# Decoder block on eight cores: spare PSUM banks for projections, more output buffers, a new memory map for one of two programs, and a shared prefix

## The chip, the cores and the metric

The kernel runs on all 8 cores of one Trainium2 chip, in one launch. Cores 0 to 3 are one die, cores 4 to 7 the other. The time is device microseconds (us) of the slowest core, as the median of several executions. In some executions one die is granted a lower TensorE clock and the run is 2 to 17% longer; such runs are slow. Means by core use fast runs alone; the plain medians include the slow runs.

## The reference

One layer on a residual stream `x` of 4 sequences of 4096 tokens and 1024 channels. Cut to what matters:

```python
u = rms_norm(x, norm_mix)
q, k, v, z, g_att, g_pool = split(u @ w_in)       # q, k, v: 24 heads of 64 each
q, k = partial_rope(q), partial_rope(k)
att = dilated_attention(q, k, v)                  # windows 128, 512, 2048 with dilations 1, 4, 16;
                                                  # groups combined by softmax denominators
pooled = multiscale_pool(z) @ w_pool_group * pool_scale
merged = sigmoid(g_att) * (att @ w_att_branch) + sigmoid(g_pool) * (pooled @ w_pool_branch)
h = x + merged @ w_out
f = rms_norm(h, norm_ffn)
h = h + (silu(f @ w_ffn_gate) * (f @ w_ffn_up)) @ w_ffn_down
return rms_norm(h, norm_final)
```

Two cores share a sequence. The even core takes tokens 0 to 2127, the odd core the other 1968, for which it recomputes keys and values of a history.

## The kernel before

The two halves are two programs, `First` (even cores) and `Second` (odd cores), each a list of instructions per engine. They are in one binary, and every engine branches on a flag at its start:

```python
def both(eng, e=e):
    v = eng.value_load(flag)
    with eng.If(v > 0):
        progs[1].body(eng, e)        # Second
    with eng.Else():
        progs[0].body(eng, e)        # First
```

The lists are written by an emitter with its own timing model. Each instruction moves its engine's modelled clock on, and the next unit of TensorE work is the one that can start first by that model. ScalarE's modelled cost:

```python
def act(out, in_, func, **kw):
    ...
    return P.op("act", ..., (width(in_) / 1200 + 0.11, 0.08))   # us busy, us until visible
```

PSUM has eight banks. During attention the scores have banks 0 to 3, the attention outputs 4 and 5, and the projections of the next head pair, which fill TensorE's gaps, only 6 and 7:

```python
pj = dict(banks=tuple(range(8)))

def bank():
    return PSB[min(pj["banks"], key=lambda i: P.ready("pe", [], [PSB[i]]))]
...
        pj["banks"] = (6, 7)                 # when scores are emitted
...
        pj["banks"] = (6, 7, 0, 1, 2, 3)     # after the last scores
```

The FFN runs in two passes over the tokens. The final norm of the first pass's tokens, and its output, are tasks that are interleaved with the second pass: `c2` takes two tasks per FFN step. The outputs go through four staging buffers:

```python
def norm_tasks(cols, sq, ps, rs, fin):
    ...
    return out + [lambda: None] * 8 + [root] + [lambda c=c: fin(cols, rs, c) for c in range(8)]

def emit_out(slots, queues=("sp",)):
    def f(cols, rs, c):
        o = slots[C["o"] % len(slots)][:, 0:cols.stop - cols.start]
        C["o"] += 1
        stt(o, ht[c][:, cols], cstv[:, 16 + c:17 + c], rs, ALU.mult, ALU.mult)
        P.outs.append(P.dma(queues[C["o"] % len(queues)], T["oT"][c * 128:(c + 1) * 128, cols], o, more=True))
    return f
...
ost = [f32(K.OST + i * K.FN, K.FN) for i in range(4)]
...
for i, cols in enumerate(FP[0]):
    tasks += norm_tasks(cols, K.SQB, PSB[4 + i % 2], rs2[i % 2], eo)
c2(1, tasks)                                 # pop(tasks, 2) after each step of 16 matmuls
```

SBUF is one tile, `arena`, cut by hand: each program is a class of offsets. [...]

The softmax here doesn't subtract the row's maximum and nothing guards it: scores larger than these inputs give would overflow.

Of the kernel before, what the change touches and what calls it, by code (L numbers as in the profile page):

```python
# [18 lines left out]
NFIRST = 2128  # L19
NW = 53152  # L20
GRAN = 32
# [4 lines left out]
class First:  # L26
# [10 lines left out]
    RPIECE = ((0, 532, 1064),) * 3  # L37
    NMSK = 2016
    GT = (432, 432, 432, 416, 416)
    FP = ((352, 352, 352), (352, 352, 368))  # L40
    TAILS = (192, 176)
    FN, PW = 368, 1072
    UTH, UTO, ATT = None, 8544, 17056
    CST, MSK, ONE = 21312, 21440, 22464
    QK = ((0, 2128, 4256), (22528, 24656, 26784)) * 2
    VS = (28912, 30544, 32176)
    ACC, ACT_ = 33808, 37904
    PT = 38064
    WP = 40112
    TAB = (44720, 45784, 46848)  # L50
    XR = (47912, 48976, 50040)
    TT = 51104
    XS = ((ATT, ATT + 2048), (ACC, ACC + 2048), (22528, 24576), (26624, 6400), (VS[2], 0))
    SQP = (PT, XR[0]) * 2 + (PT,)
    RSP0 = TT
    NTS = (6400,) * 3 + (22528,)
    POOLT = 0
    ZB, ZS, ZT16, ZRUN = 4272, 448, 8368, (45488, 45920, 46352)
    ZW, WPG, WPGS = WP, 45232, 7856
    MERGED = 28912  # L60
    HT = (4288, 6416, 22528, 24656, 26784, 46768, 48896, 51024)
    RING = (42160, 43696, 40112)
    SIGS = (38064, 39088, 46848, 47872, 48896, 49920, 50944, 51968)
    WO = (37424, 41648, MSK, MSK + 512, 45488, 46000, 40112, 40624)
    WO_LATE = 2
    ACTT, RS2, FT = 8544, 20336, 0
    WGU = (38064, 42160, 44208)
    WDX = (28912, 31728, 0, 42160)
    SQA, SQB, SQC = 17760, 34544, 2816
    SIL, OST, OSL = 36016, 40112, 38064  # L70

class Second:
# [10 lines left out]
    RPIECE = ((0, 528, 1056), (0, 576, 1152), (0, 512, 1024, 1536))  # L83
    NMSK = 1024
    GT = (496, 496, 496, 480)
# [3 lines left out]
    UTH, UTO, ATT = 0, 8192, 16384  # L89
    CST, MSK, ONE = 20480, 20608, 21120  # L90
    QK = ((21184, 23296, 29152),) * 4
    VS = (25600, 27232, 32224)
# [16 lines left out]
    RING = (43488, 45024, 41440)  # L109
    SIGS = (39392, 40416, 47008, 48032, 49056, 50080, 51104, 52128)  # L110
    WO = (37344, 37856, 38368, 38880, 27328, 27840, 28352, MSK)
# [4 lines left out]
    SQA, SQB, SQC = ACTT + 18 * 512, 27328, 2816  # L116
    SIL, OST, OSL = 29376, 30400, 43488

# [13 lines left out]
class Prog:  # L132
# [181 lines left out]

    def body(self, eng, e):
        for waits, fn, inc in self.ops[e]:
            for s, v in waits:
                eng.wait_ge(s, v)
            if fn is not None:
                ins = fn(eng)  # L320
                if inc is not None:
                    ins.then_inc(inc[0], inc[1])

def emit(nc, progs, flag):
    with nc.Block() as block:
        for e, deco in (("pe", block.tensor), ("act", block.scalar), ("dve", block.vector),
                        ("pool", block.gpsimd), ("sp", block.sync)):
            def both(eng, e=e):
                v = eng.value_load(flag)  # L329
                with eng.If(v > 0):  # L330
                    progs[1].body(eng, e)
                with eng.Else():
                    progs[0].body(eng, e)

            deco(both)
# [65 lines left out]
def _body(P, T, AR, PS, K):  # L401
    PSB = [PS[:, i * 512:(i + 1) * 512] for i in range(8)]

    def f32(off, n):
        return AR[:, off:off + n]

    def bf(off, n):
        return AR[:, off:off + n // 2].bitcast(BF16)
# [40 lines left out]
    eps = cstv[:, 96:97]  # L449
    mskv = [bf(K.MSK + i * 256, 512) for i in range(3 - K.HF)]  # L450
    onev = bf(K.ONE, 128)
# [49 lines left out]
    for i in range(2):  # L501
        load_piece(1, i)
    for k in range(2, 4):
        load_x(k)

    def load_consts(q, tabs):
# [4 lines left out]
        if 0 in tabs:  # L511
            P.dma(q, bf(K.MSK, K.NMSK), T["msk"][:, 0:K.NMSK])

    if not K.HF:
# [4 lines left out]
        load_consts("pool", (2,))  # L519
    memset(onev, 1.0)  # L520
    act(f32(K.PT, 1), onev[:, 0:1], AF.Square)
    for i in range(WARM):
        mm(PSB[7][:, 0:128], onev, onev, True, True)

    def ones(g):
# [10 lines left out]

    for g in range(2):
        ones(g)
        if K.HF:
            pads(g)  # L540

    pj = dict(banks=tuple(range(8)))

    def bank():
        return PSB[min(pj["banks"], key=lambda i: P.ready("pe", [], [PSB[i]]))]

# [3 lines left out]
    def norm(k):  # L550
# [5 lines left out]
        for a, b in K.PIECES[k]:  # L556
# [7 lines left out]
            def stat(a=a, b=b, n=n):  # L564
                ps = bank()[:, 0:n]

                def emit():
# [11 lines left out]
                    if not K.HF:  # L579
                        if k == 4:  # L580
                            ones(2)
                        return
# [227 lines left out]
    def scores(sp, qi):  # L810
# [5 lines left out]
        def finish():  # L816
            if n == 4 * NS - 1:
                pj["banks"] = (6, 7, 0, 1, 2, 3)
            done(("s", n), *[("S", sp, k) for k in closes])

        def make():
# [4 lines left out]
            def emit():  # L826
                pj["banks"] = (6, 7)
                for a, (b, pb, _) in enumerate(quad):
# [14 lines left out]
        def make_tail():  # L843
            def emit():
                pj["banks"] = (6, 7)
                for g, kb_, cols, c0_ in tail_parts():
# [6 lines left out]
                for lo, nk in ((0, 128), (240, 80)):  # L853
                    src = PS[0:nk, 0:1024].rearrange("p (e c) -> p e c", e=2)[:, :, lo:lo + 240]
                    v = pts[0][0:nk].rearrange("p (e c) -> p e c", e=2)[:, :, lo:lo + 240]
                    act(v, src, AF.Exp, scale=0.125)
                    mk = bf(K.MSK + 768, 480)[0:nk, lo:lo + 240]
                    tt(v, v, mk.unsqueeze(1).broadcast_to([nk, 2, 240]), ALU.mult)
# [206 lines left out]
    wo = [bf(o, 1024).rearrange("p (c n) -> p c n", c=8) for o in K.WO]  # L1065
    sigv = [[f32(o + k * 512, 512) for k in range(2)] for o in K.SIGS]
    sfree, sused = list(range(len(K.SIGS))), {}

# [36 lines left out]
    def load_wo(dcs):  # L1105
        for dc in dcs:
            P.dma("pool", bf(K.WO[dc], 1024), T["wout"][dc])

    def mixed(i):
        dc, tg = divmod(i, NG)  # L1110
# [21 lines left out]
    while mi < total:  # L1132
        n = 2 if gi - mi > 1 or gi == total else 1
        if gi < total:
# [7 lines left out]
        if not loaded and max(sused.values()) < 2:  # L1142
            loaded = True
            for c in range(8):
                if K.HF:
                    P.dma("sp", ht[c][:, 0:1536].rearrange("p (g t) -> p g t", g=3), xhv[c][:, 4:7, :])
                    P.dma("sp", ht[c][:, 1536:K.T], xhv[c][:, 7, 0:K.OWN[3]])
                else:
                    P.dma("sp", ht[c][:, 0:2048].rearrange("p (g t) -> p g t", g=4), xhv[c][:, 4:8, :])
                    P.dma("sp", ht[c][:, 2048:K.T], T["xt"][:, c * 80:c * 80 + 80])  # L1150
            load_wo(range(8 - K.WO_LATE))

    actt = bf(K.ACTT, NJ * K.PW).rearrange("p (j t) -> p j t", j=NJ)
# [4 lines left out]
    sil = [f32(K.SIL + i * K.FN, K.FN) for i in range(2)]  # L1158
    ost = [f32(K.OST + i * K.FN, K.FN) for i in range(4)]
    FP = [spans(K.FP[0]), spans(K.FP[1], sum(K.FP[0]))]  # L1160
# [115 lines left out]
    for i, cols in enumerate(FP[0]):  # L1276
        tasks += norm_tasks(cols, K.SQB, PSB[4 + i % 2], rs2[i % 2], eo)
    c2(1, tasks)
# [4 lines left out]
    hw = max(K.TAILS)  # L1283
    halves = [[f32(o + i * hw, hw) for i in range(8)] for o in (K.OST, K.OSL)]
    parts = FP[1][:-1] + spans(K.TAILS, FP[1][-1].start)
# [144 lines left out]
```

## Time and profile before

| | us |
|---|---|
| median of 5 runs (lowest, highest) | 1162.27 (1161.22, 1281.11) |
| spans of even cores 0, 2, 4, 6 in the profiled run | 1163.1, 1159.5, 1159.7, 1157.4 |
| spans of odd cores 1, 3, 5, 7 in the profiled run | 1155.2, 1156.5, 1156.6, 1157.8 |
| mean span over 28 fast runs in the three later sessions, even and odd cores | 1158.1 and 1157.2 |

How to read the lines: PE is TensorE's matmul side, ACT is ScalarE, DVE is VectorE, and an evacuation is a copy out of PSUM by one of these two; `SPq` is the queue on which SyncE issues transfers. A row of the time line gives start, duration, engine, source line, operation, output and input; the bracket at its end gives the idle time of the engine before it and what ended it. Most instructions go through small helpers, so a line number names the helper: L425, L434, L439, L443 and L420 before are L432, L441, L446, L450 and L427 after (ScalarE, two of VectorE, the memset, the matmul). The page's sums are of the slowest core, which is core 0 before.

### The profile page before, as it was taken

The numbers are of one execution on the slowest core, as the hardware profiler recorded it, in microseconds if no ns is written. First come the engines' busy times: TensorE is split into PE (matmuls) and PEld (weight loads), VectorE is DVE, ScalarE is ACT, GpSimd is POOL, SyncE is SP. The second block draws the span as 40 slices with busy tenths as digits, with TensorE's granted clock in tenths as the row PEclk, the third lists the DMA queues.
The fourth block names the chain that finished last, engine by engine and source line by source line (L and its number), as shares of the span: only waits on it lengthen the run. The fifth ranks groups of instructions, "written<-read, shape, count | busy, mean of one in ns | idle before, by whom it ended". The sixth has DMA issues, their size and how long they took to land.

```text
span 1163.1 us, 23864 instructions; the slowest of 8 cores (1155.2 to 1163.1 us)
## 1 busy us (share of the span) xinstructions
PE 1107.8 (95%) x9246; PEld 725.4 (62%) x9246; DVE 525.4 (45%) x918; ACT 430.4 (37%) x788; POOL 64.9 (6%) x126
## 2 busy tenths in 40 slices
PE   4999989989999999999999999999999999899997
PEld 3666649538647755555556666666666665566677
DVE  2533584553384598544347822222354342332244
ACT  2744765553763775222223221211221343231122
POOL 4020000000000000100000000000000000000000
PEclk9999999999999999999999999999999999899999
DMA  6885335155035406852103074343443454340522
GB/s 128 261 158 134 92 76 110 17 104 137 11 72 123 78 1 140 206 134 41 19 1 73 8 166 73 74 76 70 74 85 66 86 123 81 84 118 5 97 75 79
DMA packets 41736, 103.36 MB, mean 89 GB/s; under 512 B 5712, under 2 KB 13008, under 8 KB 37648
## 3 DMA queue, kind: packets, MB, share of 16 engines
q0 software_dynamic: 16992, 63.57, 29.5%
q1 hardware_dynamic: 23328, 36.89, 10.9%
q8 instruction: 78, 1.28, 0.5%
q10 hardware_dynamic: 1296, 1.28, 0.4%
q14 instruction: 42, 0.34, 0.1%
HBM read 136.67 MB, written 18.52 MB: 133 GB/s over the span
## 4 chain that ended last, share of the span: by engine, by line
PE 82%; DMA 8%; DVE 3%; issue 3%; ACT 3%; SPq 1%; POOL 0%; POOLq 0%; DVEq 0%; ACTq 0%
PE ps_all L420 82%; DVE arena L434 3%; ACT arena L425 3%; DMA arena<-wd 2%; DMA arena<-sb 1%; DMA sa<-arena 1%; DMA sb<-arena 1%; SPq L306 1%; DMA arena<-xs 1%; DMA oT<-arena 1%; DMA arena<-sa 1%; DVE arena L439 0%; POOL arena L306 0%; POOLq L329 0%; DVE arena L472 0%
## 5 line engine op out<-in xcount | busy, mean ns | idle before, releaser
L420 PE MATMUL ps_all<-arena 128*128 128x352 bf16 (+12 forms) x9246 | 1107.8, 283 | 48.5 <-ACT arena L425 25.9
L420 PEld LDWEIGHTS ps_all<-arena 128*128 128x128 bf16 (+2 forms) x9246 | 725.4, 102 | 430.8 <-issue 72.7
L425 ACT ACTIVATE arena<-ps_all 128x512 bf16<-128x512 f32 (+8 forms) x530 | 296.3, 586 | 515.0 <-PE ps_all L420 479.9
L434 DVE TENSOR_TENSOR arena<-arena 128x1024 bf16<-128x1024 bf16 (+13 forms) x334 | 220.5, 670 | 150.6 <-ACT arena L425 114.4
L434 DVE TENSOR_TENSOR arena<-ps_all,arena 128x352 bf16<-128x352 f32 (+5 forms) x220 | 129.2, 594 | 294.5 <-PE ps_all L420 294.3
L425 ACT ACTIVATE arena<-arena 128x352 f32<-128x352 f32 (+13 forms) x222 | 109.7, 512 | 123.9 <-DVE arena L434 100.3
L439 DVE SCALAR_TENSOR_TENSOR arena<-arena 128x352 bf16<-128x352 f32 (+10 forms) x183 | 88.0, 533 | 55.0 <-ACT arena L425 40.8
L439 DVE SCALAR_TENSOR_TENSOR arena<-arena,ps_all 128x432 f32<-128x432 f32 (+1 forms) x80 | 47.2, 597 | 79.9 <-PE ps_all L420 77.3
L425 ACT ACT_TABLE_LOAD x15 | 19.2, 1283 | 59.6 <-PE ps_all L420 48.6
L306 POOL DMA_DIRECT2D arena<-wgu x22 | 11.6, 528 | 372.6 <-PE ps_all L420 325.0
L306 POOL DMA_DIRECT2D arena<-wq x36 | 19.3, 546 | 221.7 <-PE ps_all L420 210.6
L439 DVE SCALAR_TENSOR_TENSOR arena<-ps_all,arena 128x352 f32<-128x352 f32 (+1 forms) x48 | 24.5, 521 | 10.0 <-PE ps_all L420 10.0
L472 DVE CAST arena<-ps_all 80x128 bf16<-80x128 f32 (+3 forms) x20 | 7.5, 374 | 32.0 <-PE ps_all L420 32.0
L306 POOL DMA_DIRECT2D arena<-wb x24 | 12.7, 532 | 162.8 <-PE ps_all L420 162.8
L425 ACT ACTIVATE arena<-ps_all,arena 128x352 f32<-128x352 f32 (+7 forms) x21 | 10.8, 514 | 28.5 <-PE ps_all L420 28.4
L1040 DVE TENSOR_TENSOR_SCAN arena<-arena 128x432 f32<-128x432 f32 (+1 forms) x15 | 16.5, 1103 | 0.9 <-ACT arena L425 0.4
L306 POOL DMA_DIRECT2D arena<-wd x8 | 4.2, 529 | 121.6 <-PE ps_all L420 121.4
L443 DVE MEMSET arena<- 128x16 f32 (+3 forms) x9 | 3.4, 379 | 7.9 <-issue 7.4
L306 POOL DMA_DIRECT2D arena<-tab x6 | 3.4, 570 | 42.5 <-DMA arena<-tab 42.5
L306 POOL DMA_DIRECT2D arena<-wout x8 | 4.2, 553 | 14.8 <-PE ps_all L420 14.8
L306 POOL DMA_DIRECT2D arena<-wz x1 | 0.5, 527 | 73.1 <-PE ps_all L420 73.1
L306 POOL DMA_DIRECT2D arena<-xT x8 | 4.3, 639 | 0.0
(11 smaller groups left out, 8.1 us busy)
## 6 DMA issues: line engine op xcount, KB each, us to landing
arena<-wgu POOLq DMA_DIRECT2D x22, 1024.0 KB, 8.1
arena<-wd POOLq DMA_DIRECT2D x8, 1408.0 KB, 11.2
arena<-wq POOLq DMA_DIRECT2D x36, 256.0 KB, 6.0
arena<-xT SPq DMA_DIRECT2D x8, 1024.0 KB, 11.6
oT<-arena SPq DMA_DIRECT2D x40, 176.0 KB, 1.9
arena<-sa SPq DMA_DIRECT2D x12, 532.0 KB, 4.2
arena<-wb POOLq DMA_DIRECT2D x24, 256.0 KB, 5.4
arena<-xT POOLq DMA_DIRECT2D x8, 512.0 KB, 26.5
```

Source lines behind the costliest of these rows:

```text
L306: self.ops[q].append((waits, lambda e: e.dma_start(out=out, in_=in_), (sem, 16)))
L420: return P.op("pe", lambda e: e.matmul(out, lhsT=lhsT, rhs=rhs, start=start, stop=stop, **kw), [lhsT, rhs], [out], (busy, 0.17))
L425: return P.op("act", lambda e: e.activation(out=out, in_=in_, func=func, **kw), rd, [out], (width(in_) / 1200 + 0.11, 0.08))
L434: return P.op("dve", lambda e: e.tensor_tensor(out=out, in0=in0, in1=in1, op=op), [in0, in1], [out], cost_dve(out, in0, in1))
L439: return P.op("dve", lambda e: e.scalar_tensor_tensor(out=out, in0=in0, scalar=scalar, in1=in1, op0=op0, op1=op1), rd, [out], (width(out) ...
L443: return P.op("dve", lambda e: e.memset(out, v), [], [out])
L472: P.op("dve", lambda e: e.tensor_copy(out=dst, in_=src), [src], [dst], cost_dve(dst, src))
L1040: P.op("dve", lambda e: e.tensor_tensor_scan(out=s, data0=z[:, 16:16 + n], data1=z[:, 16 - w:16 - w + n], initial=sl, op0=ALU.add, op1=ALU ...
```

## The change

Its intent: let projections use the score banks when these are idle; never let an output step wait for its staging buffer; make room for the added buffers by a new map of `First`; and prepare a prefix that both programs run ahead of the branch. The core of the diff, with cuts marked:

```diff
 class First:
+    MSX = 39600
-    UTH, UTO, ATT = None, 8544, 17056
+    UTH, UTO, ATT = None, 8544, 21184
 [... nearly all offsets of First move ...]
+    HT_LATE = (7,)
-    SIL, OST, OSL = 36016, 40112, 38064
+    SIL, OST = 19184, (36080, 36448, 36816, 37184, 32976, 33344, 46304)
 class Second:
-    SIL, OST, OSL = 29376, 30400, 43488
+    SIL, OST = 29376, (30400, 30912, 31424, 31936, 32448, 32960)
 [...]
             def both(eng, e=e):
+                n = progs[1].mark[e]
+                assert progs[0].mark[e] == n
+                progs[1].body(eng, progs[1].ops[e][:n])
                 v = eng.value_load(flag)
                 with eng.If(v > 0):
-                    progs[1].body(eng, e)
+                    progs[1].body(eng, progs[1].ops[e][n:])
 [...]
+    memset(onev, 1.0)
+    act(f32(NW - 1, 1), onev[:, 0:1], AF.Square)
+    for i in range(WARM):
+        if i == 20:
+            P.mark = {e: 0 for e in P.ENGS}  # again
+        mm(PSB[7][:, 0:128], onev, onev, True, True)
 [... the same warm-up is taken out further down ...]
-    for g in range(2):
-        ones(g)
-        if K.HF:
+    if K.HF:
+        for g in range(2):
+            ones(g)
             pads(g)
 [... First: ones(0) and ones(1) now after norm 0 ...]
-    pj = dict(banks=tuple(range(8)))
+    pj = dict(banks=tuple(range(8)), spare=())
     def bank():
-        return PSB[min(pj["banks"], key=lambda i: P.ready("pe", [], [PSB[i]]))]
+        when = {i: P.ready("pe", [], [PSB[i]]) for i in pj["banks"] + pj["spare"]}
+        own = min(pj["banks"], key=when.get)
+        if when[own] <= P.free["pe"] + 0.3:
+            return PSB[own]
+        return PSB[min(when, key=when.get)]
 [...]
-                pj["banks"] = (6, 7)
+                pj.update(banks=(6, 7), spare=(0, 1, 2, 3))
 [... twice; the eighth residual column of First is loaded later ...]
-    ost = [f32(K.OST + i * K.FN, K.FN) for i in range(4)]
+    ost = [f32(o, K.FN) for o in K.OST]
 [...]
-        tasks += norm_tasks(cols, K.SQB, PSB[4 + i % 2], rs2[i % 2], eo)
+        each = norm_tasks(cols, K.SQB, PSB[4 + i % 2], rs2[i % 2], eo)
+        tasks += each[:-8]
+        for step in each[-8:]:
+            tasks += [step, lambda: None]
```

## The prediction

> **What bounds the kernel now.** I read the list of cores first, then the page's slices, then the waits of the matmul engine for one core of each program, then the time line around each long wait. The kernel is two programs in one binary, chosen by a flag: even cores run `First` (the first 2128 tokens of a sequence), odd cores `Second` (the other 1968 and a history). The time is that of the slowest core.
>
> ```profile
> core 0: 1163.1 us, clock 0.993
> core 1: 1155.2 us, clock 0.992
> core 6: 1157.4 us, clock 0.991
> core 7: 1157.8 us, clock 0.990
> ```
>
> The programs end within 8 us of each other: even cores at 1157.4 to 1163.1, odd at 1155.2 to 1157.8. To lower the time both must be shortened, and the smaller of the two gains counts, less the head start of about 3 us that `Second` has.
>
> ```profile
> PE 1107.8 (95%) x9246; PEld 725.4 (62%) x9246; DVE 525.4 (45%) x918; ACT 430.4 (37%) x788; POOL 64.9 (6%) x126
> PE   4999989989999999999999999999999999899997
> PEclk9999999999999999999999999999999999899999
> ```
>
> TensorE is busy for 95% of the span, so only its idle 55 us on core 0 (41 us on core 1, which shows 1114.2 busy of 1155.2) is to be had. The digits place it: the start, the attention part (slices 5 to 14), one late dip at slice 34, where the granted clock dips too, and the tail. Waits of TensorE, core 0 and then core 1 (L425 is the helper for every ScalarE instruction, L434 and L439 two for VectorE, L443 the memset; us in total, times, longest):
>
> ```profile
> PE ps_all L420 <- ACT arena L425: 25.9, 27, 4.5
> PE ps_all L420 <- DVE arena L434: 8.7, 10, 5.2
> PE ps_all L420 <- DVE arena L443: 7.4, 1, 7.4
> PE ps_all L420 <- DMA arena<-sb: 3.6, 5, 1.1
> ...
> PE ps_all L420 <- ACT arena L425: 20.9, 20, 3.3
> ```
>
> The 5.2 us is one event. The time line of core 0:
>
> ```profile
> 978.69 14.23 SPq L306 DMA_DIRECT2D oT<-arena  x8
> ...
> 981.04 0.58 DVE L439 SCALAR_TENSOR_TENSOR arena<-arena 128x352 f32<-128x352 f32 x1
> ...
> 990.51 0.58 DVE L439 SCALAR_TENSOR_TENSOR arena<-arena 128x352 f32<-128x352 f32 x1 [8.88 <-DMA oT<-arena]
> 991.01 0.52 DVE L434 TENSOR_TENSOR arena<-ps_all,arena 128x352 bf16<-128x352 f32 x1
> 991.67 8.55 PE L420 MATMUL ps_all<-arena 128*128 128x352 bf16 x40 [5.19 <-DVE arena L434]
> ```
>
> The final norm's output steps use four staging buffers. The next one that needed a buffer waited 8.88 us for an output transfer; VectorE is in order, so the FFN product behind it (L434) waited too, and TensorE ran out of PSUM banks. All four even cores have this gap (5.19, 4.31, 4.09, 3.78 us), no odd core has. The attention waits look like this, on core 1:
>
> ```profile
> 262.71 4.03 ACT L425 ACTIVATE arena<-arena 64x512 f32<-64x512 f32 x6
> 266.64 1.00 ACT L425 ACTIVATE arena<-ps_all 128x512 bf16<-128x512 f32 x2
> 267.37 8.71 PE L420 MATMUL ps_all<-arena 128*128 128x432 bf16 x112 [2.19 <-ACT arena L425]
> ...
> 274.75 4.03 ACT L425 ACTIVATE arena<-arena 64x512 f32<-64x512 f32 x6 [1.55 <-DVE arena L434]
> 278.68 1.07 ACT L425 ACTIVATE arena<-ps_all 128x512 bf16<-128x512 f32 x2
> 279.40 60.76 PE L420 MATMUL ps_all<-arena 128*128 128x128 bf16 x766 [3.33 <-ACT arena L425]
> ```
>
> Six Ln/Exp instructions of the division stand in ScalarE's queue ahead of two PSUM copies. During attention projections own only banks 6 and 7, so TensorE waits until the copies have run, while banks 0 to 3 (the scores') are empty.
>
> **What the Trainium skill says.** "TensorE: Matmul & The Clock Gate", section "Why this matters for your kernels": matmul bursts should not be more than about 3 us apart, or the clock falls to half. The trace agrees: after the 5.19 us gap the stretch 991.6 to 995.0 shows clock 0.50 and 12 matmuls, where 3.4 us normally hold 23. "Perfetto Trace Analysis", section "Matmuls": independent matmul groups should rotate through PSUM banks so that the evacuation of one lies beside the next. The two-bank gaps above are that case. "DMA: Bandwidth & Descriptors", section "Issuing engines are not separate DMA queues": all issuers share the same engines and interleave. The output transfers land in 1.6 us at least, 1.9 at the median and 10.8 at most; the slow ones began at 978.69, right behind a 1 MB weight load issued at 978.56, which fits. "Runtime: NRT & Kernel Launch", section "Instruction fetch mechanics": a taken branch to a far target forces an instruction fetch. Here VectorE's first memset runs at 7.08 us on core 0 (the else branch) against 2.68 on core 1, which fits as well.
>
> **The change part by part.**
>
> (1) A shared prefix of the two programs ahead of the branch. The emitter now splits each program at a mark, but the mark is set to zero for every engine, so the prefix is empty and the branch stays where it was. The warm-up moves up in the source only; DMA issue is in another stream, so on VectorE, ScalarE and TensorE the order is as before. Worth 0 us. The even cores keep their late start: their first useful ScalarE square is at 16.09 us against 6.62.
>
> (2) `Spare` banks: when both own banks would be late by over 0.3 us in the emitter's own timing, a projection takes the earliest of banks 0 to 3. Core 1's long waits on ScalarE between 160 and 400 us are 1.80, 1.32, 2.19, 3.33, 2.19 and 3.34, in sum 14.2 us. On core 0 the time line gives 5.2 (five of the six between 0.5 and 1.4) at the first boundary, then 2.9, 2.7 and 3.7, in sum 14.4 us in smaller pieces. A 512-column projection is 8 matmuls of some 0.22 us, 1.8 us; four more banks cover 7.2 us, longer than any of these gaps. I do not count all of it: work pulled forward is missing as filler later, scores then find a bank still occupied, and choices rest on modelled times. Estimate: two thirds on odd cores, 9 us; somewhat over half on even cores, 8 us, because many of their waits are of 0.5 us, near the threshold.
>
> (3) Output buffers 4 to 7 (`First`) and 4 to 6 (`Second`), and one output step per FFN step in the second FFN pass in place of two. An FFN step is 16 matmuls of 0.149, 2.4 us, so a buffer of `First` comes round after 7 x 2.4 = 16.7 us against the longest 10.8 us landing: the wait is gone. Worth on even cores: 83 matmuls ran from 980 to 1000 us on core 0 against 134 in the 20 us before; 51 missing at 0.149 is 7.6 us (5.2 idle and 2.4 at the low clock). Cores 2, 4, 6 ran 93, 95, 97: 6.1, 5.8, 5.5 us. The added empty tasks must fit: 3 x 40 = 120 tasks in 66 x 2 = 132 places in `First`, 2 x 40 = 80 in 88 in `Second`, so nothing is left to spill at the end. Odd cores: 0 us.
>
> (4) `First`'s new memory map. The projection weights, ring, PSUM-fed buffers and FFN weights move by constant amounts or keep their order in the queue. The first two down weights leave the merged tile's place, but sit behind the third gate weight in the same queue, which waits for the output projection anyway: 0 us. The third and fourth down weights still wait for the end of the second FFN pass; the 0.7 us wait there stays. The eighth residual column is loaded only after the last gate: about 2.8 us of mixing and 9.4 us of output projection pass before it is wanted, against an estimate of 7 to 8 us for 1.1 MB: hidden. The two memsets of the value tiles (0.96 us each, at 7.42 and 8.56, when VectorE was free) must now wait until the first input tile has been consumed, near 43.7 us, just ahead of the second tile's scaling, which TensorE takes up at 47.6: up to 1.9 us of delay, I take 1 us lost.
>
> Sums. Core 0: 1163.1 - 7.6 - 8 + 1 = 1148.5. Other even cores: 1157.4 to 1159.7 less about 6 and 8, plus 1: 1144 to 1147. Odd cores: 1155.2 to 1157.8 less 9: 1146 to 1149. The slowest is near 1149; the clocked time of the profiled run was 1.6 us above its longest span, so 1151.
>
> **The rivals.** First, the spare banks give little: evacuation order, not banks, could be the limit. For it: VectorE and ScalarE run back to back in those stretches, and the next head pair's rope, not a projection, releases the next scores. Against: on core 1 TensorE is 100% busy from 280 to 340, so there is filler in plenty. Then odd cores stay at 1157 and the time is 1157 to 1159. Second, the spare banks give all 14 us, with less left for the rope chains: odd cores 1143, even 1142 to 1144, the time 1145. Third, occupied score banks delay the scores by more than is gained: 1160 to 1165; against it, scores come first in the emitter's order and a spare is taken only when no score was ready. Fourth, the prefix is meant to work and the start falls by up to 9 us on even cores; with the mark at zero I give this no weight, and odd cores would not follow.
>
> **Range and chances.** The odd cores decide, with a gain from 1 to 14 us: 1144 to 1158 holds it 8 times in 10, with 1151 in the middle. Faster by over 2% needs 1139.0, 23 us less, more than the known waits of `Second` allow: 0.03. Slower by over 2%: 0.01. Within 2%: 0.96.
>
> **What would show it.** The stretch 980 to 1000 us (shifted) with about 134 matmuls and clock 1.00 on even cores confirms (3); any VectorE wait on an output transfer of several us refutes it. TensorE's wait on ScalarE falling from 20.9 to about 10 us on core 1 and from 25.9 to about 17 on core 0 confirms (2); the same idle time moved to waits on VectorE or on the rope transfers is the first rival. VectorE's first memset still at 7 us on core 0 confirms (1). I am wrong if the even cores start earlier, or if a new wait appears at the output projection or at the reloaded down weights.

## The result, and the profile after

The changed kernel gives the right result. Its median is 1151.87 us (1149.28 to 1217.97, 8 runs), against 1162.27 (1160.01 to 1281.11, 15 runs) of the kernel before. The ratio is 0.9906, with a 95% interval of 0.9896 to 0.9917. Ratios here are the mean time of one kernel's fast runs over the mean of the other's fast runs of the same rounds, so not quite the ratio of the medians. It is a gain of 0.9%: within 2%, measurably faster.

The list of cores after (span, mean granted clock):

```profile
core 0: 1142.2 us, clock 0.992
core 1: 1151.8 us, clock 0.991
...
core 6: 1144.4 us, clock 0.997
core 7: 1151.0 us, clock 0.990
```

The order has turned: `First` now ends 4 to 10 us before `Second`. Over nine fast runs after, the even cores average 1144.0 us and the odd ones 1148.5, which is 14.1 and 8.7 us below the means before (1158.1 and 1157.2 over 28 fast runs in the three later sessions). The time is the slowest core's, so 5 us of what `First` gained isn't in it.

The 40 slices of core 0 after, from the page of that core:

```profile
PE   4999989999998999999999999999999999999997
PEclk7999999999999999999999999999999999999999
```

Against before, the dip at slice 34 is gone from both rows. The attention part still shows two eights (slices 5 and 12, before 5 and 8), and the first slice still has a 4: the late start is as it was. The first digit of the clock, 7 here and 9 before, is that of the start and differs between cores and runs. Waits of TensorE, core 0 and then core 1 (us in total, times, longest):

```profile
PE ps_all L427 <- ACT arena L432: 19.9, 20, 3.1
PE ps_all L427 <- DVE arena L450: 6.8, 1, 6.8
PE ps_all L427 <- DMA arena<-sb: 3.3, 4, 2.2
...
PE ps_all L427 <- ACT arena L432: 12.0, 19, 1.6
PE ps_all L427 <- DMA arena<-sb: 3.1, 5, 1.3
```

The wait on ScalarE fell from 25.9 to 19.9 us on core 0 and from 20.9 to 12.0 on core 1 (on cores 3, 5 and 7 from 19.6 to 21.5 before to 11.9 to 12.7). On core 1 a part of that came back: 2.2 us as waits on the rope transfers (`arena<-sb`, the rotated rows of queries and keys on their way back from memory: 0.9 before, 3.1 after), and 1.6 us as a new wait on VectorE's copies out of PSUM (L479). In these two profiles core 1 is only 3.4 us shorter (1155.2 to 1151.8), so the mean of 8.7 can't be read from this one core. The 6.8 us on the memset is the start, 7.4 before. The time line of core 1 at the two boundaries that the prediction showed:

```profile
262.55 4.03 ACT L432 ACTIVATE arena<-arena 64x512 f32<-64x512 f32 x6
...
266.49 1.49 ACT L432 ACTIVATE arena<-ps_all 128x512 bf16<-128x512 f32 x3
...
267.21 10.49 PE L427 MATMUL ps_all<-arena 128*128 128x432 bf16 x144 [0.46 <-ACT arena L432]
...
279.27 2.44 PE L427 MATMUL ps_all<-arena 128*128 128x128 bf16 x40 [1.57 <-ACT arena L432]
```

Before, the two waits were 2.19 and 3.33 us; now they are 0.46 and 1.57. Each became shorter by 1.73 to 1.76 us, which is one projection (8 matmuls of some 0.22 us). The emitter put exactly one projection into each gap; the 3.33 us had room for nearly two.

The late gap of core 0: busy times by engine between 980 and 1000 us, before and after (PE, PEld, DVE, ACT, POOL, then clock, DMA share and GB/s):

```profile
980.00:1000.00 20.00, 14.81 (x83) 8.69 (x82) 5.99 (x13) 4.26 (x10) 0.00 (x0) 0.83 0.55 117
```

```profile
980.00:1000.00 20.00, 20.00 (x135) 12.96 (x133) 8.07 (x17) 5.65 (x13) 1.05 (x2) 1.00 0.64 133
```

TensorE is busy throughout, with 135 matmuls at full clock instead of 83 at 0.83. On the even cores no instruction waits for an output transfer any more, though the slowest still took 9.2 us to land (10.8 before).

To see where the time went, I used the issue times of the eight down-weight loads as marks. The first comes at the end of the output projection, but not at the same place with both maps: it goes out 15.25 us before the fourth gate weight of the pass with the old map of `First` and 13.80 us before it with the new one, so ends of the output projection are compared only between runs of one map. The third comes after the first of four down blocks of the first FFN pass; between the sixth and the seventh lie all gate and up products of the second pass, in which the late gap was. Means of the four even cores of the profiled runs:

| even cores, us | before | after | difference |
|---|---|---|---|
| third load issued | 844.7 | 834.1 | -10.6 |
| third to sixth load | 59.4 | 59.4 | 0.0 |
| sixth to seventh load (second pass, gate and up) | 166.6 | 159.95 | -6.65 |
| rest to the end | 89.3 | 89.4 | +0.1 |
| span | 1159.9 | 1142.9 | -17.0 |

The start of a core scatters by 1 to 2 us between runs (first ScalarE square of an even core at 15.4 to 16.1 us before, 14.0 to 17.7 after), and this one run of before was slower than the mean of many, 1158.1. So the second pass's 6.65 is firm (165.8 to 167.5 before, 159.95 on all four cores after), while the 10.6 holds some scatter. On odd cores the output projection ends at 704.2 before and 697.7 after, and what follows takes 452.3 and 452.4 us.

### The profile page after: what moved, and what is told of

It is laid out like the page before; its sums are of the slowest core, which is core 1 after, so compare pages of the same core. It is cut to its first block, busy times and chain, and to the rows that moved or that the text cites. A ratio compares the mean times of both kernels' runs of the same rounds, so it can differ in the third digit from the quotient of the medians.

```text
span 1151.8 us, 21536 instructions; the slowest of 8 cores (1142.2 to 1151.8 us)
## 1 busy us (share of the span) xinstructions
PE 1116.6 (97%) x8417; PEld 648.5 (56%) x8417; DVE 523.4 (45%) x786; ACT 447.7 (39%) x711; POOL 69.0 (6%) x134
## 3 DMA queue, kind: packets, MB, share of 16 engines
q8 instruction: 71, 1.16, 0.4%
## 4 chain that ended last, share of the span: by engine, by line
PE 82%; DMA 7%; DVE 5%; ACT 2%; issue 2%; SPq 1%; POOL 0%; POOLq 0%; DVEq 0%; ACTq 0%
PE ps_all L427 82%; DVE arena L441 4%; ACT arena L432 2%; DMA sb<-arena 2%; DMA arena<-sb 2%; DMA sa<-arena 2%; SPq L310 1%; DMA arena<-sa 1%; DMA arena<-xs 1%; DVE arena L446 1%; POOL arena L310 0%; POOLq L336 0%; DVEq L322 0%; ACTq L322 0%; SPq L322 0%
## 5 line engine op out<-in xcount | busy, mean ns | idle before, releaser
L427 PE MATMUL ps_all<-arena 128*128 128x128 bf16 (+7 forms) x8417 | 1116.6, 296 | 24.1 <-ACT arena L432 12.0
L427 PEld LDWEIGHTS ps_all<-arena 128*128 128x128 bf16 (+1 forms) x8417 | 648.5, 105 | 492.0 <-issue 39.8
L432 ACT ACTIVATE arena<-ps_all 128x512 bf16<-128x512 f32 (+8 forms) x491 | 309.7, 660 | 499.3 <-PE ps_all L427 493.5
L441 DVE TENSOR_TENSOR arena<-arena 128x1024 bf16<-128x1024 bf16 (+11 forms) x308 | 224.7, 745 | 159.6 <-ACT arena L432 132.5
L441 DVE TENSOR_TENSOR arena<-ps_all,arena 128x496 bf16<-128x496 f32 (+4 forms) x160 | 114.9, 728 | 295.7 <-PE ps_all L427 281.9
L432 ACT ACTIVATE arena<-arena 128x512 f32<-128x512 f32 (+8 forms) x187 | 114.7, 631 | 124.9 <-DVE arena L441 104.6
L446 DVE SCALAR_TENSOR_TENSOR arena<-arena 128x512 bf16<-128x512 f32 (+6 forms) x172 | 99.4, 632 | 40.8 <-ACT arena L432 39.6
L446 DVE SCALAR_TENSOR_TENSOR arena<-arena,ps_all 128x496 f32<-128x496 f32 (+1 forms) x64 | 42.0, 665 | 75.7 <-PE ps_all L427 75.3
L310 POOL DMA_DIRECT2D arena<-wgu x22 | 11.6, 529 | 300.6 <-PE ps_all L427 242.5
L446 DVE SCALAR_TENSOR_TENSOR arena<-ps_all,arena 128x496 f32<-128x496 f32 (+1 forms) x32 | 21.1, 665 | 12.3 <-PE ps_all L427 12.2
L310 POOL DMA_DIRECT2D arena<-wb x24 | 12.7, 532 | 171.2 <-PE ps_all L427 171.2
L432 ACT ACTIVATE arena<-ps_all,arena 128x512 f32<-128x512 f32 (+5 forms) x20 | 11.9, 596 | 27.1 <-PE ps_all L427 27.0
L479 DVE COPY arena<-ps_all 128x512 f32<-128x512 f32 x12 | 8.3, 691 | 23.5 <-PE ps_all L427 23.4
L310 POOL DMA_DIRECT2D arena<-xT x24 | 12.7, 570 | 47.4 <-DVE arena L446 45.9
L1054 DVE TENSOR_TENSOR_SCAN arena<-arena 128x496 f32<-128x496 f32 (+1 forms) x12 | 14.9, 1246 | 1.3 <-ACT arena L432 1.0
L479 DVE CAST arena<-ps_all 128x256 bf16<-128x256 f32 (+2 forms) x9 | 2.8, 306 | 9.2 <-PE ps_all L427 9.1
## 6 DMA issues: line engine op xcount, KB each, us to landing
arena<-xT POOLq DMA_DIRECT2D x24, 512.0 KB, 19.9
arena<-wd POOLq DMA_DIRECT2D x8, 1408.0 KB, 10.3
arena<-xs POOLq DMA_DIRECT2D x6, 512.0 KB, 15.3
```

The source lines that it names most:

```text
L310: self.ops[q].append((waits, lambda e: e.dma_start(out=out, in_=in_), (sem, 16)))
L427: return P.op("pe", lambda e: e.matmul(out, lhsT=lhsT, rhs=rhs, start=start, stop=stop, **kw), [lhsT, rhs], [out], (busy, 0.17))
L432: return P.op("act", lambda e: e.activation(out=out, in_=in_, func=func, **kw), rd, [out], (width(in_) / 1200 + 0.11, 0.08))
L441: return P.op("dve", lambda e: e.tensor_tensor(out=out, in0=in0, in1=in1, op=op), [in0, in1], [out], cost_dve(out, in0, in1))
L446: return P.op("dve", lambda e: e.scalar_tensor_tensor(out=out, in0=in0, scalar=scalar, in1=in1, op0=op0, op1=op1), rd, [out], (width(out) ...
L479: P.op("dve", lambda e: e.tensor_copy(out=dst, in_=src), [src], [dst], cost_dve(dst, src))
```

## The experiments

The leading theory: the spare banks shorten the attention part of both programs, the output part takes the late gap out of `First` alone, and everything else is worth about nothing. Rivals: the parts depend on each other (a staging buffer's wait hides or feeds another wait), the memory map or the prefix does something, or the choice of spare banks is limited by something else than the model. Ten kernels were run, all correct. One table for all, with mean spans over fast runs:

| kernel | even, us | odd, us | median, us | ratio to before (95%) |
|---|---|---|---|---|
| before | 1157.6 to 1158.7 | 1157.2 to 1157.3 | 1161.83 to 1163.21 | 1 |
| changed | 1144.0 | 1148.5 | 1151.87 | 0.9906 (0.9896 to 0.9917) |
| `e1_spare_only` | 1154.8 | 1148.1 | 1159.67 | 0.9960 (0.9938 to 0.9981) |
| `e2_no_spare` | 1150.1 | 1157.0 | 1161.87 | 0.9984 (0.9963 to 1.0005) |
| `e3_buf_only` | 1144.1 | 1148.6 | 1152.67 | 0.9909 (0.9881 to 0.9937) |
| `e4_space_only` | 1142.4 | 1148.8 | 1151.41 | 0.9898 (0.9873 to 0.9924) |
| `e5_prefix` | 1150.0 | 1151.3 | 1156.62 | 0.9945 (0.9925 to 0.9966) |
| `e6_late_ones` | 1157.5 | 1157.7 | 1162.82 | 1.0008 (0.9977 to 1.0039) |
| `e7_thr0` | 1142.0 | 1148.3 | 1151.55 | 0.9922 (0.9895 to 0.9950) |
| `e8_cost` | 1137.2 | 1149.0 | 1153.73 | 0.9929 (0.9909 to 0.9949) |
| `e9_mixed` | 1138.5 | 1147.7 | 1151.33 | 0.9904 (0.9888 to 0.9921) |
| `e10_cost_nospare` | 1167.3 | 1163.1 | 1171.16 | 1.0066 (1.0046 to 1.0087) |

The row "before" gives the range over the three sessions in which the others ran; means of different sessions are to be compared with its 1.1 us in mind. `e3`, `e4` and `e6` rest on two runs each. Slow were three of seven runs of `e1`, two of six of `e2`, three of eight of `e5` and one of four of `e10`, which lifts these medians.

### e1_spare_only: the kernel before with the spare banks alone

```diff
+        when = {i: P.ready("pe", [], [PSB[i]]) for i in pj["banks"] + pj["spare"]}
+        own = min(pj["banks"], key=when.get)
+        if when[own] <= P.free["pe"] + 0.3:
+            return PSB[own]
+        return PSB[min(when, key=when.get)]
 [...]
-                pj["banks"] = (6, 7)
+                pj.update(banks=(6, 7), spare=(0, 1, 2, 3))
 [... twice ...]
```

> The kernel before with the spare banks alone (both programs), old memory map, four output buffers, two output steps per FFN step. Main theory: the two parts add up, the spare banks give all of the odd cores' gain and most of the even cores' gain ahead of the FFN. Odd cores 1149 to 1152 us as in the changed kernel (before 1155 to 1158); even cores 1159.9 - 10 = about 1150, still with the 4 to 5 us gap near 975 us; the time 1151 to 1154. Rival A (the memory map or the wider output buffers gave part of the gain ahead of the FFN): even cores fall by under 7 us, to 1153 or more, and lead the time. Rival B (the spare banks are worth nothing, the evacuation order is the limit): odd cores stay at 1155 to 1158.

Measured: the odd cores have the whole of their gain (1148.1, against 1157.2 in the same session). The even cores don't:

```profile
core 0: 1155.6 us, clock 0.986
core 1: 1144.9 us, clock 0.995
...
core 4: 1158.1 us, clock 0.984
```

Their output projection ends at 658.6 in the mean, 7.8 us earlier than before. But the second FFN pass takes 167.3 to 169.3 us, where before it took 165.8 to 167.5, and the rest to the end is 1.4 us longer, with a wait on the reloaded down weights of up to 2.1 us on core 4. So of 7.8 us won, about 3 are given back later, and over all fast runs 3.9 us are left. Who waits for the output transfers, on core 0 of this kernel (us, times):

```profile
  DVE arena L439: 13.8, 3
```

It is the gap of the kernel before, 12.6 us there. With it, the even cores set the time, and the odd cores' 9 us buy only the 0.4% of the table. The main theory's 1150 for the even cores is missed by 5 us. Rival A has the end right (even cores at 1153 or more, leading the time) but not its reason: ahead of the FFN the gain is whole, and what is lost is lost later.

### e2_no_spare: the changed kernel without the spare banks

```diff
-                pj.update(banks=(6, 7), spare=(0, 1, 2, 3))
+                pj.update(banks=(6, 7), spare=())
```

> The changed kernel with the list of spare banks left empty, so that only the memory map, the output buffers and their spacing are left. Main theory: odd cores as before, 1155 to 1158 us, and they set the time at 1156 to 1160; even cores lose only the output gap, 5.5 to 7.6 us, and 0.7 us of the down-weight wait: 1152 to 1154. Rival A (the memory map helps ahead of the FFN as well): even cores at 1150 or less, with the output projection reached before 664 us (before 664.8 to 667.9). Late memsets cost 1 us as predicted: even cores up to 1154.5.

Measured: the mirror image. The second FFN pass takes 159.85 us, the even cores gain 8.6 us in the mean against the same session, and the odd cores stay at 1157.0. The time doesn't move (0.9984, the interval holds 1), since the odd cores now set it. Two of its six runs were slow, so its median of 1161.87 is a little high for fast runs. The even cores ended below the 1152 to 1154 of the main theory. Rival A is not shown by it: the new map's mark lies later in the work (see the table of marks), and by the third load this run is 2.0 us ahead of before (842.6 against 844.7), no more than `e6_late_ones` with the old map (842.4). The two parts together are worth 0.9%, each alone 0.4% and 0.2%, the latter not clear of zero: a maximum over two programs falls only when both fall.

### e3_buf_only and e4_space_only: two remedies for one wait

```diff
 e3: more buffers, two output steps per FFN step as before
-        tasks += each[:-8]
-        for step in each[-8:]:
-            tasks += [step, lambda: None]
+        tasks += each
 e4: one output step per FFN step, four buffers as before
-    ost = [f32(o, K.FN) for o in K.OST]
+    ost = [f32(o, K.FN) for o in K.OST[:4]]
```

> The changed kernel with the seven and six output buffers but without the empty steps, so two output steps per FFN step as before. Worked out from the trace: seven buffers come round after 3.5 FFN steps of 2.4 us, 8.4 us, and the slowest landing was 9.2 to 10.8 us, so a wait of at most 1 to 3 us of VectorE is left and TensorE, with two more PSUM pairs of work ahead of it, hardly stops: even cores within 1.5 us of the changed kernel (1142 to 1146). Rival (the spacing does the work because the transfers are slow only when eight are issued at once): TensorE shows a gap of over 2 us in the second FFN pass on even cores and they end at 1146 to 1150. Odd cores unchanged at 1149 to 1152, so the time stays near 1152 in both.

> The changed kernel with four output buffers but with the empty steps, so one output step per FFN step. Four buffers come round after 4 x 2.4 = 9.6 us against a slowest landing of 9.2 to 10.8 us: a VectorE wait of 0 to 1.5 us, no TensorE gap over 1 us, even cores within 1 us of the changed kernel. If so the spacing alone would have been enough. Rival (buffers do the work): VectorE waits over 3 us on an output transfer and TensorE shows a gap on even cores. Odd cores unchanged at 1149 to 1152.

Measured: the second FFN pass takes 159.85 us with buffers alone and 159.95 with spacing alone, on all even cores. The sixth load of down weights and the two after it on core 0 of `e3_buf_only`, 159.85 us apart:

```profile
893.46 0.53 POOL L310 DMA_DIRECT2D arena<-wd  x1 [19.32 <-PE ps_all L427]
1053.31 1.05 POOL L310 DMA_DIRECT2D arena<-wd  x2 [42.60 <-PE ps_all L427]
```

VectorE waits for output transfers for 0.3 us at most with buffers alone and 0.4 to 0.9 us with spacing alone, in sum for a core, while the slowest transfer still takes 9.4 to 10.3 and 8.5 to 9.5 us to land. Either remedy by itself takes the whole gap out, and having both adds nothing that these runs can tell (two runs each).

### e5_prefix: the prefix that the change prepares, switched on

```diff
-            P.mark = {e: 0 for e in P.ENGS}  # again
+            P.mark = {e: len(P.ops[e]) for e in P.ENGS}  # again
```

> The changed kernel with the mark set to the number of instructions emitted so far, so that the shared prefix (first loads, memset, table load, 20 of the 45 warm-up matmuls) is really issued ahead of the flag's branch. Main theory (the prefix was worth nothing because it was empty, and the late start of the even cores is the branch): VectorE's first memset on even cores moves from about 7 us to below 3.5 us and the first ScalarE square from 14 to 17.7 us to 8 to 11 us; even cores end 4 to 8 us earlier, at 1135 to 1140; odd cores, which set the time, stay at 1147 to 1152, so the time stays within 2 us of the changed kernel's 1151.9. Rival (the instruction fetch stall only moves into the warm-up and then delays the next loads): even cores gain under 2 us.

Measured: the first memset now runs at 1.16 us on every core and the first 20 warm-up matmuls at 1.47 us. Yet nothing useful comes earlier. ScalarE and TensorE of core 0, from the time line:

```profile
2.85 0.20 ACT L432 ACTIVATE arena<-arena 128x1 f32<-128x1 bf16 x1
...
13.96 1.28 ACT L432 ACT_TABLE_LOAD   x1 [10.91 <-issue]
15.25 1.15 ACT L432 ACTIVATE arena<-arena 128x512 bf16<-128x512 f32 x2
16.47 3.28 PEld L427 LDWEIGHTS ps_all<-arena 128*128 128x128 bf16 x33 [12.98 <-issue]
16.47 3.45 PE L427 MATMUL ps_all<-arena 128*128 128x128 bf16 x33 [12.71 <-issue]
```

The engines stand still for 10.9 and 12.7 us behind the prefix, waiting for nothing that the profile shows. Before, ScalarE of core 0 reached its first issue of a transfer at 6.60 us, stayed in it for 4.12, and ran its first instruction at 10.81. So on an even core the way through the branch costs ScalarE about as much behind the prefix (10.9 us) as at the start (10.8); the prefix only puts it later. The second table load, 1.28 us, comes on top. On the odd core 1, which takes the other branch, the stall is 6.1 and 8.8 us, where without the prefix ScalarE issues its first transfer at 2.50 us, and its first square slips from 6.7 to 10.5 us. Neither expectation came: no first square of an even core at 8 to 11 us (15.3 to 17.6), and a loss instead of a gain. Against the changed kernel the even cores lose 6.0 us and the odd 2.8. So the late start of an even core goes with the branch and not with the place of the warm-up. What the stall is made of (the fetch of instructions, the load of the flag, the transfers under way) these runs don't separate, and why the even cores lose more than the odd was not pursued.

### e6_late_ones: the kernel before with First's memsets moved late

```diff
-    for g in range(2):
-        ones(g)
-        if K.HF:
+    if K.HF:
+        for g in range(2):
+            ones(g)
             pads(g)
 [...]
                     if not K.HF:
-                        if k == 4:
-                            ones(2)
+                        for g in {0: (0, 1), 4: (2,)}.get(k, ()):
+                            ones(g)
```

> The kernel before with one thing changed: the two memsets of the value tiles on even cores are issued after the first input tile has been scaled, as the changed kernel must do. Prediction's theory: up to 1.9 us of delay on VectorE at about 44 us, TensorE loses about 1 us: TensorE shows a new wait of 0.5 to 2 us between 42 and 50 us on even cores. Rival (TensorE has other units to run, so nothing is lost): no wait over 0.4 us there, and the output projection ends at 664 to 668 us as before, apart from the start's own scatter of 2 us. The time stays at 1160 to 1164.

Measured: no wait of TensorE on a memset between 36 and 62 us, only the two of 0.40 and 0.35 us on ScalarE that the kernel before has too. But that window holds no memset. VectorE of core 0 has them earlier than was expected:

```profile
30.41 0.96 DVE L443 MEMSET arena<- 128x1088 bf16 x1 [0.18 <-issue]
31.55 0.96 DVE L443 MEMSET arena<- 128x1088 bf16 x1 [0.18 <-issue]
```

There VectorE has nothing else to do (it then idles for 6.31 us until 38.83), and TensorE runs without a wait from 24.78 to 39.42 us. In the changed kernel they are at 30.46 and 31.60. So the two memsets delay nobody; the end of the even cores, 1157.5 against 1157.6 in the same session, agrees, though two runs alone could not tell 1 us.

### e7_thr0: the threshold for a spare bank set from 0.3 us to 0

```diff
-        if when[own] <= P.free["pe"] + 0.3:
+        if when[own] <= P.free["pe"]:
```

> The changed kernel with the threshold for a spare bank at 0 instead of 0.3 us of lateness of the own banks. The emitted program of the odd cores uses a spare bank 22 times instead of 21, that of the even cores 44 times instead of 47. Main theory (the threshold is not what limits the gain): odd cores 1147 to 1152, time within 1.5 us of the changed kernel. Rival (many waits of about 0.5 us sit under the threshold, as the prediction assumed for the even cores): even cores gain 2 us or more, to 1141 or less.

Measured: 1142.0 and 1148.3. The odd cores and the time are as the main theory had it. The even cores are 2.0 us below those of the changed kernel, just the rival's 2 us, but short of its 1141; `e4_space_only`, which leaves the attention part as it is, is 1.5 us below too, so a small gain is neither shown nor excluded. Spare uses in the emitted programs: 47 in `First` and 21 in `Second` in the changed kernel, 44 and 22 here. The threshold is not what keeps the second projection out of the long gaps.

### e8_cost: a dearer ScalarE in the emitter's model

The model gives a ScalarE instruction of 512 columns 512/1200 + 0.11 = 0.54 us. In the trace the six Ln/Exp of a division take 4.03 us, 0.67 each, and a copy from PSUM lasts 0.596 us. The copies overlap, however: those back to back start 0.48 to 0.50 us apart, so the raised cost is nearer to the trace for Ln and Exp and for a copy alone, but not for copies in a row.

```diff
-                    (width(in_) / 1200 + 0.11, 0.08))
+                    (width(in_) / 1200 + (0.24 if func in (AF.Ln, AF.Exp) and width(in_) <= 512 else 0.16), 0.08))
```

> The changed kernel with ScalarE's modelled duration raised to what the trace shows: Ln and Exp of 512 columns 0.67 us instead of 0.54 us, others by 0.05 us. In the changed kernel each long wait behind a division on odd cores shrank by just one projection (2.19 to 0.46 and 3.33 to 1.57 us), and the emitted program took one spare bank there; with the longer model it takes a spare bank 31 times instead of 21 on odd cores. Main theory (the optimistic model of ScalarE held the gain below the 14 us in reach): the 1.57 us waits near 279 and 383 us fall below 0.5 us, odd cores gain 3 to 5 us more, to 1144 to 1147, and the time to 1146 to 1149. Rival (work pulled forward is missing later): the waits shrink there but others grow between 400 and 480 us, and odd cores stay at 1147 to 1152. Even cores may change by 2 us either way (35 spare picks instead of 47).

Measured: the even cores gain another 6.8 us in the mean, to 1137.2, where 2 us either way had been expected. The odd cores don't gain (1149.0), so the 3 to 5 us of the main theory didn't come. Waits of TensorE on core 1:

```profile
PE ps_all L427 <- ACT arena L432: 7.7, 15, 1.6
PE ps_all L427 <- DMA arena<-sb: 7.1, 5, 3.2
```

The wait on ScalarE fell from 12.0 to 7.7 us, and the waits at 267, 279, 371 and 383 us are gone, as the main theory had it. But the wait on the rope transfers rose from 3.1 to 7.1, with 3.22 us at 390 us. Work drawn forward into the gaps is missing as filler when the rope data of the next head pair is late. For `Second` the rival holds: the idle time changed its name. The time got a little worse, as the odd cores vary more (1144.6 to 1155.4 in the profiled run, 1148.7 to 1151.8 in that of the changed kernel).

### e9_mixed: the dearer model for First alone

```diff
-                    (width(in_) / 1200 + 0.11, 0.08))
+                    (width(in_) / 1200 + (0.11 if K.HF else 0.24 if func in (AF.Ln, AF.Exp) and width(in_) <= 512 else 0.16), 0.08))
```

> The changed kernel with the raised ScalarE cost of the earlier cost run for First alone; Second keeps the emitter's old cost and so, by the emitted program, the same 21 spare uses as in the changed kernel. Main theory (the two programs are independent and the slower one sets the time): even cores end near 1134 to 1138 as in the cost run, odd cores at 1147 to 1151 as in the changed kernel, and the time stays at 1149 to 1152, a ratio of 0.989 to 0.992: 6 us taken off First buy nothing. Rival (the cores share the chip's memory, so cores that run ahead disturb or relieve the others): odd cores move by more than 3 us against 1147 to 1150, either way.

Measured: even cores 1138.5, odd cores 1147.7, time 1151.33, ratio 0.9904. `First` is 5.5 us shorter than in the changed kernel and the time is the same. From the list of cores:

```profile
core 0: 1137.1 us, clock 0.995
core 1: 1146.3 us, clock 0.993
...
core 7: 1148.1 us, clock 0.993
```

It shows that `Second` alone sets the time after the change, and that a faster `First` doesn't disturb it by anything near 3 us. This is not a better version than the changed kernel, only one with more slack on even cores. Single even cores scatter more than was expected: from 1132.8 to 1146.2 over the five runs, six of twenty above 1140. Core 4 of the profiled run, at 1146.2, has 4.3 us of waits on rope transfers where core 0 has none.

### e10_cost_nospare: the dearer model without spare banks

```diff
-                    (width(in_) / 1200 + 0.11, 0.08))
+                    (width(in_) / 1200 + (0.24 if func in (AF.Ln, AF.Exp) and width(in_) <= 512 else 0.16), 0.08))
-                pj.update(banks=(6, 7), spare=(0, 1, 2, 3))
+                pj.update(banks=(6, 7), spare=())
```

> The cost run without spare banks: raised ScalarE cost in the emitter for both programs, projections kept to their own two banks during attention. It fills the fourth cell of a table of spare banks (yes, no) by cost (old, raised). If the 6 us that the raised cost gained on even cores come from better choices of spare banks, then without spare banks the even cores' output projection ends at 664 to 668 us, as without spare banks at the old cost (665.8). If they come from the other choices that rest on modelled times (the order of the evacuations and which unit runs next), it ends near 658 to 661. Odd cores: near 703 (old cost without spare banks 703.1) under both.

Measured: both expectations missed. The even cores' output projection ends at 680.8 to 683.3, 16 us later than at the old cost, and the odd cores' at 709.3 to 711.1, 7 us later. The four cells, mean spans:

| even / odd, us | old cost | raised cost |
|---|---|---|
| without spare banks | 1150.1 / 1157.0 | 1167.3 / 1163.1 |
| with spare banks | 1144.0 / 1148.5 | 1137.2 / 1149.0 |

Waits on ScalarE on core 0, the longest at 8.1 us:

```profile
PE ps_all L427 <- ACT arena L432: 36.0, 28, 8.1
```

The model's cost and the banks aren't additive. With two banks the raised cost makes the order worse; with spare banks it makes `First` better. The worth of the spare banks on `First` is 6 us under the one order and 30 under the other. That the emitted order matters this much is shown; which choice in the order does it is not.

## Why the prediction was right

The predicted time was 1151.0, and 1151.87 was measured, inside the range. By its own steps:

- **The bound.** That two programs must both fall and the smaller gain counts is shown twice over: by `e1_spare_only` and `e2_no_spare`, which each shorten one program by about 9 us and leave 0.2 to 0.4% of time, and by `e9_mixed`. That the odd cores would decide is what came. The head start of about 3 us that was given to `Second` was the scatter of one run: in the mean of many it is under 1 us.
- **(1), the prefix.** Worth 0, as predicted: the first memset of core 0 runs at 6.37 us (7.08 before), and no even core starts earlier as a rule. The prediction gave no weight to a working prefix; `e5_prefix` shows that it would have cost time.
- **(2), the spare banks.** On odd cores 9 us were predicted and 8.7 to 9.1 measured. The waits on ScalarE fell to 12.0 where "about 10" was said, and on core 0 to 19.9 where it was 17. Of 8.9 us of waits on ScalarE on core 1, 2.2 came back as waits on the rope transfers and 1.6 on VectorE's copies, the sign that was named for the first rival; it came in part, and it is a loss for which the "two thirds" allowed. The prediction named modelled times as a reason in general. That ScalarE's cost in the model keeps the emitter at one projection for a gap is what `e8_cost` shows; that occupied score banks delayed scores is not shown by any run. On even cores 8 us were predicted. At the end of the output projection it is 7.8 (`e1_spare_only` against before) and 8.5 (the changed kernel against `e2_no_spare`, 657.3 to 665.8), both of single runs; over all fast runs the ends differ by 6.1 us (1150.1 to 1144.0, two sessions). So the 8 us were too much by 2 for the time. That 3 us are given back when the spare banks stand alone was not foreseen.
- **(3), the output part.** Predicted 5.5 to 7.6 us on even cores and 0 on odd; measured 6.65 in the second FFN pass and 0. The prediction didn't say that buffers or spacing alone would do, which `e3_buf_only` and `e4_space_only` show.
- **(4), the memory map.** The 1 us loss from the late memsets was wrong, and so was its reason: they were placed near 43.7 us, just ahead of a scaling, and ran at 30.4 us, where VectorE was idle (`e6_late_ones`). No new wait came at the output projection (one of 0.3 us on core 0, before and after). The 7 to 8 us for the late residual column named no source; loads of 1 MB on the page before land in 8.1 us (gate weights) and 11.6 us (residual columns) at the median, still under the 12.2 us that it had. The map alone was not run. The 0.7 us wait on the reloaded down weights was said to stay and is gone after the change on core 0; that is a small miss.
- **The sum.** For even cores the prediction's 1148.5 and 1144 to 1147 come to some 13 us of gain in the mean, and 14.1 were measured. That is partly luck, for errors cancel: the spare banks give 2 us less than was said (6.1), and what is left without them, 8.6 us in `e2_no_spare`, is some 3 more than parts (3) and (4) promised. Of the 8.6 the second pass accounts for some 6.7 and the end, where the down weights' wait is gone, for 0.4; the rest may be the scatter of the start and is not settled. For the time it made no difference, as the odd cores set it.

Of the rivals, the first (spare banks give little) and the third (they cost more than they give) are refuted by `e1_spare_only`, the second (all 14 us) by the 12.0 us of waits left on core 1. The fourth (a prefix that works) didn't arise: with the mark at zero no even core starts earlier. What stays open is whether tokens could be moved from `Second` to `First` to use the 5 to 9 us of slack. The split of 2128 tokens has a tail of 80 that is written into buffers and tables by hand, so it was not tried.

## What to carry to other kernels

Where several programs or cores must finish together, list the gain of each part for each of them, and then take the maximum of the ends: two good parts can each look worthless alone. When an in-order engine waits for a buffer, look at what stands behind it in its queue; here an output step without a free buffer stopped TensorE, and either more buffers or fewer steps at a time was enough. A scheduler that picks by modelled times should be held against the trace's durations, but costs nearer to the trace needn't give a better order: measure it with the resource limits that it will really have.

## What the Trainium skill lacked or had wrong

- "Runtime: NRT & Kernel Launch", section "Instruction fetch mechanics", says that a taken branch outside the fetched window stalls until its target is fetched, and gives no size. The stall behind the prefix of `e5_prefix`, which fits that description (the profile names it only as issue), is 10.9 us on ScalarE and 12.7 us on TensorE in the else branch, and 6.1 and 8.8 us in the other. The 20 warm-up matmuls ahead of it, 2.3 us in all, did not hide it.
- "TensorE: Matmul & The Clock Gate", section "Why this matters for your kernels", tells to expect the 13/16 clock (0.81) when three or more cores of a die are busy. Here eight cores with random data are 95% busy on TensorE, and every fast run has a mean granted clock of 0.98 to 1.00. Slow runs do fall towards it, for one die: 0.811 to 0.833 on cores 0 to 3 in one run of `e2_no_spare` of 1361.97 us, with 0.99 on the other die. So it is a state of some runs, not the rule.
- "ScalarE: Activation LUTs", section "What ACT_TABLE_LOAD costs", gives 186 ns + 0.833 ns per column for an activation with immediate scale and bias, 613 ns at 512 columns, and an overlap of about 93 ns back to back. The trace agrees on one instruction (596 ns from PSUM, 628 ns for the Ln/Exp from SBUF). But nothing overlaps in a division's six (two Ln and one Exp, twice, from SBUF to SBUF), which take 4.03 us: they start 0.65 us apart, and 0.72 where the Exp waits for the Ln that it reads. Copies from PSUM do overlap, by about what the page says: of those in a row, lasting 0.58 us, the next starts after 0.48 to 0.50. The page doesn't tell the two cases apart.
